# Gate copies placed together ahead of U loads, an uneven split of U tiles around a stage border, and the value stationary tiles in another pool

## The chip, the cores and the metric

One core of one Trainium2 chip. The metric is the device time of one execution in microseconds; times given for runs are medians of several executions.

## What is computed

One residual block over 512 tokens of width 1024, in float32. With RMSNorm in front of each part:

```
p  = xn @ W_in                        # 7 sections of 1024 columns
x  = x + W_out(sigmoid(ma)*ya + sigmoid(mb)*yb)      # two gated token mixers
q  = xn @ W_q ; top 16 of 128 sub-keys twice per head, top 16 of their sums   # 8 heads
x  = x + sum over the 128 chosen experts e of  g_e * gelu(<xn, U[e]>) * V[e]
out = RMSNorm(x)
```

There are 128 x 128 experts; U and V are tables of 16384 rows of 1024 floats (64 MB each). The changed part is the last sum.

## The kernel before

Tokens stand in four tiles of 128. The first token tile is done by gathering rows of U and V with indirect DMAs. The other three tiles (`NDT` = 3, 384 tokens) are done densely: for all 128 blocks of 128 experts, TensorE makes hidden values with U (**U tiles**, psum `ph`, function `h_mm`, lines 396 to 400), a gate matrix says which experts a token chose and with which weight, and TensorE multiplies gated hidden values with V (**V tiles**, psum `acc`, `v_mm`, lines 824 to 833).

A float32 product is made of three fp32r products: each operand is split in a rounded part (`hi`, ScalarE copy) and the rest (`lo`, a subtraction on VectorE), and hi\*hi, hi\*lo, lo\*hi are added (`mm3`, lines 144 to 149). A matrix product has a stationary operand, loaded into the array, and a moving one. In the tables of a profile the names behind `<-` are both. For `pin`, `pq`, `ph` the stationary tile is the weight (`hi_in`, `hi_q`, `hi_u` and their `lo`) and the normed input `a1h`, `a1l` moves; for `po` the merged mixers `mh`, `ml` are stationary, for `pgt` `waxh`, `waxl`; for `acc` `wh`, `wl` (384 columns, used 128 at a time) are stationary and `hi_v`, `lo_v` move.

**Pools.** A tile pool is a stretch of each partition. `const` and `strm` are made first and lie lowest; `fp` (stage 1), `gp`, `ha`, `qp`, `sp`, `op`, `dp` come above. `strm` holds `raw` (6 buffers, `RB`), `hi` and `lo` (3 each, `SB`). `wh` and `wl` (3 each, lines 844, 845) are in `dp`, near the end. The first two weight tiles of W_q are split into `strm`, the other fourteen into `qp` (line 500). In the built program the `strm` splits lie at bytes 78,912 to 103,488 of a partition, those of `qp` at 138,944 to 163,520, `mh` and `ml` at 129,504 to 162,272, `waxh` and `waxl` at 127,296 to 129,344, `wh` and `wl` at 207,488 to 216,704.

**The stage of the gate matrices** (lines 753 to 783). For each dense token tile `t_`, 8 steps: each step (`h_step(mid)`) starts a load of a U tile if fewer than `RB` raws are out, splits one U tile if fewer than `SB` are split, and in between (`mid`) makes 16 token columns of gate matrices on TensorE (`gate_mm`, psum `pg`), which ScalarE copies to `stg` (line 731), and one-hots for the next step on VectorE (`one_hot`); then one split U tile is multiplied (`h_run`) and its result goes through gelu (`hg`) and to DRAM (`hd`, line 406). `stg` has one buffer of 8 MB. Before the next token tile may write it, it must be copied to `gd` in DRAM: four DMAs of 2 MB in pieces of 512 bytes (line 776). Behind the 8 steps stand `HB[t_]` = 6 steps without gates, so that TensorE has work meanwhile; at each of the first four, one copy is started, then the step's load. The third tile is not copied (`HB` = 0); V tiles read it in `stg`. PE, ACT, DVE and POOL keep the order written (`pinned`); the DMA queue of SP is ordered by the tile framework. A DMA started on SP waits for what it needs, and all behind it on SP wait too.

**The stage of V tiles** (lines 838 to 869). 128 turns; each loads `raw_v`, splits it (ACT, then DVE `lo_v`), loads gates `gt` and, for the last 54, stored hidden values `hr`, makes `wf` (two products on DVE), `wh` (ACT), `wl` (DVE) and 18 matmuls. The first 68 turns also make a U tile of 24 matmuls. Gathers for the first token tile run along: ACT writes the index (`eix`, line 669), POOL issues the gather (line 364), DVE adds the row block (line 387). Order here is the framework's.

## Time and profile before

| | |
|---|---|
| median of 3 runs | 1645.08 us (1640.75 to 1645.50) |
| the profiled execution | 1639.71 us |
| its span, first to last instruction | 1637.9 us |
| TensorE (PE) busy | 1610.1 us, 98% |
| VectorE busy | 1266.4 us, 77% |
| ScalarE busy | 689.4 us, 42% |
| mean granted TensorE clock | 0.994 of full speed |
| gate stage, about | 565 to 795 us of the span |
| V stage, about | 800 us to the end |

Matmuls overlap: the profile's mean duration of one is longer than the distance from one start to the next, so distances are read from the starts in the timeline. `SPq`, `ACTq` are DMA starts on those queues; the time of such a row is how long the queue was held by the start. [...] "L812 <- X" names what ended a wait.

### The profile page before, as it was taken

The page shows a single profiled execution, that of the slowest core. Times are in us where ns is not written, and L with a number is a line of the kernel's source. Part 1 is how long each engine was busy: PE and PEld are TensorE (multiplying, and loading weights), DVE is VectorE, ACT ScalarE, POOL GpSimd, SP SyncE. Part 2 cuts the span into 40 slices and gives each one's busy share as a digit, 9 for nine tenths or more (in the row PEclk, how much of TensorE's full clock was granted, in tenths as well). Part 3 has the DMA queues.
Part 4 walks back from the last instruction along what each step waited for, and adds up shares of the span by engine and source line. Part 5 has one row for each costly group of instructions (what it writes and reads, how often), then busy time and mean ns, then how long its engine had stood idle before and what let it go on. Part 6 is the DMA issues. An engine that isn't in the chain of part 4 may idle for free.

```text
span 1637.9 us, 23565 instructions
## 1 busy us (share of the span) xinstructions
PE 1610.1 (98%) x8402; PEld 1415.1 (86%) x8402; DVE 1266.4 (77%) x2404; ACT 689.4 (42%) x1222; POOL 515.2 (31%) x379
## 2 busy tenths in 40 slices
PE   9999999999999999898999999999999999999997
PEld 8888888888899999898988888999888888788775
DVE  6666666636999996767788888888888888867767
ACT  7444444434333454444434333433343333433334
POOL 0000000004788820000044544545454444223331
PEclk9999999999999999999999999999999999999999
DMA  6222323334333357777499999999999999988883
GB/s 226 93 93 94 93 94 100 98 102 179 110 123 102 128 185 229 250 239 248 165 329 329 323 328 333 334 325 330 343 325 329 328 333 354 321 305 292 289 294 142
DMA packets 157878, 378.31 MB, mean 231 GB/s; under 512 B 14016, under 2 KB 78016, under 8 KB 157632
## 3 DMA queue, kind: packets, MB, share of 16 engines
q1 hardware_dynamic: 112544, 229.86, 41.3%
q0 software_dynamic: 36864, 134.23, 23.2%
q10 hardware_dynamic: 8352, 12.72, 2.2%
q8 instruction: 65, 1.06, 0.3%
q14 instruction: 53, 0.43, 0.1%
HBM read 345.17 MB, written 31.59 MB: 230 GB/s over the span
## 4 chain that ended last, share of the span: by engine, by line
PE 73%; issue 8%; DVE 7%; DMA 6%; POOL 4%; ACT 1%; SPq 0%; POOLq 0%; DVEq 0%; ACTq 0%
PE ph L147 9%; PE ph L149 9%; PE ph L148 9%; PE pin L149 6%; PE pin L147 6%; PE pin L148 6%; PE acc L830 6%; PE acc L833 6%; PE acc L829 6%; POOL rv L364 3%; DMA rv<-in_v_tab_dram,eix 3%; PE pq L147 2%; PE pq L149 2%; PE pq L148 2%; DMA gd<-stg 1%
## 5 line engine op out<-in xcount | busy, mean ns | idle before, releaser
L147 PE MATMUL ph<-a1h,hi_u 128*128 128x384 f32 x1024 | 347.1, 339 | 0.0
L149 PE MATMUL ph<-a1h,lo_u 128*128 128x384 f32 x1024 | 344.1, 336 | 0.4 <-POOL lo_u L108 0.4
L148 PE MATMUL ph<-a1l,hi_u 128*128 128x384 f32 x1024 | 343.3, 335 | 0.0
L830 PE MATMUL acc<-lo_v,wh 128*128 128x512 f32 x768 | 303.3, 395 | 3.6 <-DVE lo_v L108 3.5
L829 PE MATMUL acc<-hi_v,wh 128*128 128x512 f32 x768 | 303.2, 395 | 0.0
L364 POOL DMA_INDIRECT rv<-in_v_tab_dram,eix x128 | 170.3, 1331 | 271.2 <-ACT eix L669 230.8
L833 PE MATMUL acc<-hi_v,wl 128*128 128x512 f32 x768 | 242.8, 395 | 0.0
L364 POOL DMA_INDIRECT ru<-in_u_tab_dram,eix x120 | 164.0, 1366 | 218.9 <-ACT eix L669 182.1
L387 DVE SCALAR_TENSOR_TENSOR acc<-rv,w,acc 128x1024 f32<-128x1024 f32 x128 | 164.6, 1286 | 86.8 <-DMA rv<-in_v_tab_dram,eix 86.4
L107 ACT ACTIVATE hi_v<-raw_v 128x1024 fp32r<-128x1024 f32 x128 | 134.7, 1053 | 189.8 <-PE ph L148 177.2
L373 DVE SCALAR_TENSOR_TENSOR ru<-ru,t 128x1024 f32<-128x1024 f32 x128 | 155.5, 1223 | 58.7 <-DMA ru<-in_u_tab_dram,eix 58.2
L148 PEld LDWEIGHTS ph<-a1l,hi_u 128*128 128x128 f32 x1024 | 193.1, 189 | 3.2
L147 PEld LDWEIGHTS ph<-a1h,hi_u 128*128 128x128 f32 x1024 | 193.1, 189 | 3.1
L149 PEld LDWEIGHTS ph<-a1h,lo_u 128*128 128x128 f32 x1024 | 192.8, 188 | 0.7 <-POOL lo_u L108 0.7
L849 ACT ACTIVATE wh<-wf 128x384 fp32r<-128x384 f32 x128 | 67.0, 525 | 276.6 <-PE acc L830 185.1
L830 PEld LDWEIGHTS acc<-lo_v,wh 128*128 128x128 f32 x768 | 143.9, 187 | 38.5 <-DVE lo_v L108 6.9
L149 PE MATMUL pin<-a1h,lo_in 128*128 128x512 f32 x448 | 174.4, 389 | 0.3 <-POOL lo_in L108 0.3
L833 PEld LDWEIGHTS acc<-hi_v,wl 128*128 128x128 f32 x768 | 143.8, 187 | 35.5 <-DVE wl L850 0.3
L148 PE MATMUL pin<-a1l,hi_in 128*128 128x512 f32 x448 | 174.4, 389 | 0.0
L147 PE MATMUL pin<-a1h,hi_in 128*128 128x512 f32 x448 | 174.3, 389 | 0.0
L829 PEld LDWEIGHTS acc<-hi_v,wh 128*128 128x128 f32 x768 | 143.8, 187 | 32.1 <-ACT hi_v L107 0.2
L108 DVE TENSOR_TENSOR lo_v<-raw_v,hi_v 128x1024 fp32r<-128x1024 f32 x128 | 156.1, 1219 | 2.4 <-ACT hi_v L107 2.3
(199 smaller groups left out, 2475.5 us busy)
## 6 DMA issues: line engine op xcount, KB each, us to landing
raw_u<-in_uT_dram SPq DMA_DIRECT2D x128, 512.0 KB, 5.4
raw_v<-in_v_tab_dram SPq DMA_DIRECT2D x128, 512.0 KB, 5.9
raw_in<-in_w_in_dram SPq DMA_DIRECT2D x56, 512.0 KB, 3.4
gd<-stg SPq DMA_DIRECT2D x8, 2048.0 KB, 12.1
gt<-gd SPq DMA_DIRECT2D x128, 128.0 KB, 5.2
hd<-hg ACTq DMA_DIRECT2D x54, 192.0 KB, 2.5
hr<-hd SPq DMA_DIRECT2D x54, 192.0 KB, 5.4
raw_q<-in_w_q_dram SPq DMA_DIRECT2D x16, 512.0 KB, 3.2
```

What stands on the lines that cost most here:

```text
L107: act.activation(hi, raw, AF.Copy)
L108: lo_eng.tensor_tensor(lo, raw, hi, op=ALU.subtract)
L147: pe.matmul(pt, wh(k), xh(k), start=start and m == 0, stop=False)
L148: pe.matmul(pt, wh(k), xl(k), start=False, stop=False)
L149: pe.matmul(pt, wl(k), xh(k), start=False, stop=stop and m == n - 1)
L364: ins = pool.indirect_dma_start(out=rows, out_offset=None, in_=tab, in_offset=bass.IndirectOffsetOnAxis(ap=ix, axis=0))
L373: dq.append(lambda: dve.scalar_tensor_tensor(rows, rows, 1.0, t0, op0=ALU.mult, op1=ALU.mult, accum_out=d0[:, n:n + 1]))
L387: dq.append(lambda: dve.scalar_tensor_tensor(acc0, rows, w0[:, n:n + 1], acc0, op0=ALU.mult, op1=ALU.add))
L829: pe.matmul(accs[t][h], wh[:, ts], hi[:, hsl], start=first, stop=False)
L830: pe.matmul(accs[t][h], wh[:, ts], lo[:, hsl], start=False, stop=False)
L833: pe.matmul(accs[t][h], wl[:, ts], hi[:, hsl], start=False, stop=last)
L849: act.activation(wh, wf, AF.Copy)
```

## The change

Loads of U tiles are topped up to six raws from step 3 on (before: step 4) and again behind the 8 steps; then the four copies of `stg` are written one behind the other, ahead of the six steps without gates, and no more inside them. The first step of token tiles 1 and 2 splits no U tile; step 3 splits up to two. `wh` and `wl` are taken from `strm` instead of `dp`; by that the built program has them at bytes 103,488 to 112,704, and what lies above `strm` moves up by 9,216 bytes (the splits of `qp` to 148,160, `mh` and `ml` to 138,720, `waxh` to 136,512).

```diff
-        def h_step(mid):
+        def h_step(mid, splits=1):
             if len(raws) < RB:
                 h_load()
-            made = None
-            if len(nxt) < SB and raws:
+            made = []
+            while len(made) < splits and len(nxt) + len(made) < SB and raws:
                 k_, raw = raws.pop(0)
                 hi = strm.tile([P, D], F32R, tag="hi", name=f"hi_u{k_}", bufs=SB)
                 act.activation(hi, raw, AF.Copy)
-                made = k_, raw, hi
+                made.append((k_, raw, hi))
             mid()
-            if made:
-                k_, raw, hi = made
+            for k_, raw, hi in made:
                 lo = strm.tile([P, D], F32R, tag="lo", name=f"lo_u{k_}", bufs=SB)
...
-                if s2 >= 4 and len(raws) < RB:
+                if s2 >= 3 and len(raws) < RB:
                     h_load()
-                h_step(mid)
+
+                h_step(mid, 0 if t_ and s2 == 0 else 2 if s2 == 3 else 1)
                 gather_steps(GSTEP[(sub // 2) % len(GSTEP)], 2)
+            while t_ < NDT - 1 and len(raws) < RB:
+                h_load()
+            if t_ < NDT - 1:
+                for q4 in range(4):
+                    sl = slice(q4 * 32, (q4 + 1) * 32)
+                    sync.dma_start(gd[sl, :, t_ * P:(t_ + 1) * P].rearrange("i j t -> j i t"), stg[:, sl, :])
             for m in range(HB[t_]):
-
-                if m < 4:
-                    sl = slice(m * 32, (m + 1) * 32)
-                    sync.dma_start(gd[sl, :, t_ * P:(t_ + 1) * P].rearrange("i j t -> j i t"), stg[:, sl, :])
                 h_step(lambda: None)
...
-        wh = dp.tile([P, TD], F32R, tag="wh", name=f"wh{i}", bufs=3)
-        wl = dp.tile([P, TD], F32R, tag="wl", name=f"wl{i}", bufs=3)
+        wh = strm.tile([P, TD], F32R, tag="wh", name=f"wh{i}", bufs=3)
+        wl = strm.tile([P, TD], F32R, tag="wl", name=f"wl{i}", bufs=3)
```

The DMA queue of SP behind the first token tile, before (`stg0` is that tile's gate matrix, `raw_u112` the load of U tile 112; U tiles run from 74 to 127, then from 0):

```order
L101 DMA raw_u111_5886<-in_uT_dram 128x1024
L776 DMA gd_2933<-stg0_5302 128x32x128
L101 DMA raw_u112_5969<-in_uT_dram 128x1024
L776 DMA gd_2933<-stg0_5302 128x32x128
L101 DMA raw_u113_6004<-in_uT_dram 128x1024
L776 DMA gd_2933<-stg0_5302 128x32x128
L101 DMA raw_u114_6039<-in_uT_dram 128x1024
L776 DMA gd_2933<-stg0_5302 128x32x128
L101 DMA raw_u115_6074<-in_uT_dram 128x1024
L101 DMA raw_u116_6108<-in_uT_dram 128x1024
```

and with the change:

```order
L101 DMA raw_u111_5886<-in_uT_dram 128x1024
L777 DMA gd_2933<-stg0_5302 128x32x128
L101 DMA raw_u112_5968<-in_uT_dram 128x1024
L777 DMA gd_2933<-stg0_5302 128x32x128 x3
L101 DMA raw_u113_6006<-in_uT_dram 128x1024
L101 DMA raw_u114_6040<-in_uT_dram 128x1024
L101 DMA raw_u115_6074<-in_uT_dram 128x1024
L101 DMA raw_u116_6108<-in_uT_dram 128x1024
```

The loads of tiles 113 and 114 no more stand between copies; the load of 112, which waits for the buffer of tile 106, still stands behind the first. Behind the second token tile it is the same, with tiles 126, 127 and 0.

ScalarE's order from the last step without gates into the next token tile, before:

```order
L404 ACTIVATE hg110_6173<-ph110_6148 128x384
L406 DMA hd_2932<-hg110_6173 128x384
L742 ACTIVATE hi_u113_6179<-raw_u113_6004 128x1024
L731 ACTIVATE stg1_6176<-pg16_0_6181 128x128x4
L731 ACTIVATE stg1_6176<-pg16_1_6191 128x128x4
L731 ACTIVATE stg1_6176<-pg17_0_6201 128x128x4
L731 ACTIVATE stg1_6176<-pg17_1_6211 128x128x4
L404 ACTIVATE hg111_6256<-ph111_6231 128x384
L406 DMA hd_2932<-hg111_6256 128x384
L742 ACTIVATE hi_u114_6261<-raw_u114_6039 128x1024
```

and with the change:

```order
L404 ACTIVATE hg110_6173<-ph110_6148 128x384
L406 DMA hd_2932<-hg110_6173 128x384
L731 ACTIVATE stg1_6176<-pg16_0_6179 128x128x4
L731 ACTIVATE stg1_6176<-pg16_1_6189 128x128x4
L731 ACTIVATE stg1_6176<-pg17_0_6199 128x128x4
L731 ACTIVATE stg1_6176<-pg17_1_6209 128x128x4
L404 ACTIVATE hg111_6252<-ph111_6227 128x384
L406 DMA hd_2932<-hg111_6252 128x384
L742 ACTIVATE hi_u113_6255<-raw_u113_6006 128x1024
```

The split of tile 113 stands one step later, behind the first copies out of psum; with step 3 the order is one tile ahead again. The orders of PE and POOL are the same before and after, and so are those of ACT and DVE outside these steps but for the first two turns of the V stage.

## Rows read from the trace of the kernel before

**Rows 1.** The page's first part: busy time of TensorE, its share of the span, instructions.
```profile
PE 1610.1 (98%) x8402; PEld 1415.1 (86%) x8402; DVE 1266.4 (77%) x2404; ACT 689.4 (42%) x1222; POOL 515.2 (31%) x379
```

**Rows 2.** TensorE's groups of instructions by line, shapes kept apart: fp32r matmuls of 512 columns in four places of the program. Behind the bar: busy us, mean ns of one, idle before them.
```profile
L147 PE MATMUL pin<-a1h,hi_in 128*128 128x512 f32 x448 | 174.3, 389 | 0.0
...
L829 PE MATMUL acc<-hi_v,wh 128*128 128x512 f32 x768 | 303.2, 395 | 0.0
...
L147 PE MATMUL po<-hi_out,mh 128*128 128x512 f32 x64 | 25.2, 394 | 0.0
...
L147 PE MATMUL pgt<-xch,waxh 128*128 128x512 f32 x16 | 6.3, 396 | 0.0
```

**Rows 3.** TensorE's timeline (start us, duration us): the first and the 16th of a run of matmuls of W_q tile 1 (split in `strm`), the first and the 19th of one of a later tile (split in `qp`), and the first matmul of V turns 68 and 69, which are 18 matmuls apart.
```profile
390.15 0.39 PE L147 MATMUL pq<-a1h,hi_q 128*128 128x512 f32 x1
...
393.55 0.39 PE L147 MATMUL pq<-a1h,hi_q 128*128 128x512 f32 x1
...
422.89 0.39 PE L147 MATMUL pq<-a1h,hi_q 128*128 128x512 f32 x1
...
427.07 0.40 PE L147 MATMUL pq<-a1h,hi_q 128*128 128x512 f32 x1
...
1371.91 0.39 PE L829 MATMUL acc<-hi_v,wh 128*128 128x512 f32 x1
...
1376.11 0.39 PE L829 MATMUL acc<-hi_v,wh 128*128 128x512 f32 x1
```

**Rows 4.** TensorE's waits, the gate stage (560 to 800 us) and the V stage (800 us to the end): us in total, times, longest.
```profile
PE pg L728 <- ACT stg L731: 12.2, 2, 6.2
...
PE acc L830 <- DVE lo_v L108: 3.5, 4, 1.5
```

**Rows 5.** TensorE's timeline around its two long waits: first and last of 16 gate matmuls, the first gate matmul behind each wait, and a U matmul behind each (7th and 8th of its tile).
```profile
664.53 0.24 PE L728 MATMUL pg<-o,oij 128*128 128x128 f16 x1
...
665.41 0.22 PE L729 MATMUL pg<-o,oij 128*128 128x128 f16 x1
671.86 0.27 PE L728 MATMUL pg<-o,oij 128*128 128x128 f16 x1 [6.23 <-ACT stg L731]
...
675.55 0.37 PE L147 MATMUL ph<-a1h,hi_u 128*128 128x384 f32 x1
...
753.39 0.27 PE L728 MATMUL pg<-o,oij 128*128 128x128 f16 x1 [5.97 <-ACT stg L731]
...
757.40 0.41 PE L148 MATMUL ph<-a1l,hi_u 128*128 128x384 f32 x1
```

**Rows 6.** Windows: behind the first wait, and the first turns of the V stage without U tiles, in which the wait of 1.5 us of rows 4 lies.
```profile
670.00:675.00 5.00, 3.14 (x21) 3.14 (x21) 1.22 (x1) 3.33 (x6) 0.00 (x0) 0.50 0.96 319
...
1370.00:1410.00 40.00, 38.88 (x170) 31.27 (x170) 33.72 (x58) 14.36 (x29) 13.26 (x11) 1.00 0.99 371
```

**Rows 7.** The timeline of SP's DMA queue behind the first token tile: start, how long the start held the queue.
```profile
631.60 0.38 SPq L776 DMA_DIRECT2D gd<-stg  x1
...
640.94 7.93 SPq L101 DMA_DIRECT2D raw_u<-in_uT_dram  x1
648.92 1.20 SPq L776 DMA_DIRECT2D gd<-stg  x1
...
659.03 1.07 SPq L776 DMA_DIRECT2D gd<-stg  x1
```

**Rows 8.** ScalarE's timeline: the gelu of two U tiles running one behind the other, and the first copies of the next token tile's gates, which waited for the copies to DRAM, behind token tiles 0 and 1.
```profile
654.49 0.49 ACT L404 ACTIVATE hg<-ph 128x384 f32<-128x384 f32 x1 [2.20 <-PE ph L149]
...
658.65 0.49 ACT L404 ACTIVATE hg<-ph 128x384 f32<-128x384 f32 x1 [2.15 <-PE ph L149]
...
671.21 2.06 ACT L731 ACTIVATE stg<-pg 128x512 f32<-128x512 f32 x4 [10.54 <-DMA gd<-stg]
...
752.74 2.07 ACT L731 ACTIVATE stg<-pg 128x512 f32<-128x512 f32 x4 [10.29 <-DMA gd<-stg]
```

**Rows 9.** Windows while the copies run (last column: GB/s of the DMA engines): two in the middle of copies, one where a load follows a copy, one at the start of the first copy behind token tile 1.
```profile
644.00:650.00 6.00, 6.00 (x37) 6.00 (x36) 2.44 (x2) 1.55 (x2) 0.00 (x0) 1.00 1.13 351
...
660.00:662.00 2.00, 2.00 (x19) 2.00 (x17) 1.97 (x3) 0.67 (x1) 0.00 (x0) 1.00 1.02 195
...
714.00:720.00 6.00, 6.00 (x37) 6.00 (x36) 5.22 (x6) 1.93 (x3) 1.61 (x1) 1.00 0.90 273
...
726.00:734.00 8.00, 8.00 (x49) 8.00 (x48) 2.23 (x2) 3.04 (x4) 0.00 (x0) 1.00 1.12 361
```

**Rows 10.** The page's DMA issues: KB of one, median us from start to landing.
```profile
gd<-stg SPq DMA_DIRECT2D x8, 2048.0 KB, 12.1
...
hd<-hg ACTq DMA_DIRECT2D x54, 192.0 KB, 2.5
```

**Rows 11.** GpSimd's timeline in the V stage without U tiles: the first gather of each group of three (turns 96, 104, 108, 112, 116; a group belongs to four turns).
```profile
1483.17 3.56 POOL L364 DMA_INDIRECT rv<-in_v_tab_dram,eix  x1 [6.50 <-ACT eix L669]
...
1516.77 3.50 POOL L364 DMA_INDIRECT rv<-in_v_tab_dram,eix  x1 [7.46 <-ACT eix L669]
...
1533.61 3.62 POOL L364 DMA_INDIRECT rv<-in_v_tab_dram,eix  x1 [7.51 <-ACT eix L669]
...
1551.28 3.62 POOL L364 DMA_INDIRECT rv<-in_v_tab_dram,eix  x1 [8.37 <-ACT eix L669]
...
1568.64 3.62 POOL L364 DMA_INDIRECT rv<-in_v_tab_dram,eix  x1 [8.11 <-ACT eix L669]
```

## The prediction

> **What bounds the kernel now.** First the busy times: TensorE is busy 98% of the span [rows 1]; nothing else comes near. So time can come only from TensorE waiting less, or from its matmuls following each other faster. Its waits by stage show where the first is to be had: in the gate stage it waits 12.2 us in two waits, both for ScalarE's copy into `stg`; in the V stage 3.5 us in four, for `lo_v` [rows 4]. Then the groups by line for the second: matmuls of one form, fp32r with 512 columns, take 389 ns in the first stage and 394 to 396 ns in three other places [rows 2]. These durations overlap, so the timeline's starts give the true distance: 15 steps of W_q tile 1 take 3.40 us, 226.7 ns each; 18 steps of a later W_q tile 4.18 us, 232 ns; a V turn of 18 takes 4.20 us, 233 ns [rows 3]. I make the sum against the profiled execution's own 1639.7 us, which lies 5.4 below the median of the runs and 1.0 below the lowest.
>
> **The copies, and what waits for them.** ScalarE's first copy of the next token tile begins at 671.21 and 752.74, each released by the DMAs from `stg` [rows 8]; TensorE goes on 0.65 us later, at 671.86 and 753.39 [rows 5]. It had stopped at 665.5 and some 747.2, with all six psum buffers for gates full: waits of 6.23 and 5.97 us. Behind each it runs at the lower clock: the window granted 0.50 [rows 6]. The 16 gate matmuls and 6 U matmuls from 671.86 to 675.55 took 3.69 us. At full clock 16 gate matmuls take 0.94 (664.53 to 665.41 is 15 steps [rows 5]) and a U matmul 0.173 (a tile of 24 each 4.16 us [rows 8]), together 1.98, so 1.7 us are lost; likewise 753.39 to 757.40, 16 and 7, 4.01 instead of 2.15, so 1.9. The two places cost 12.2 + 3.6 = **15.8 us**.
>
> How much earlier do the copies land? They are 2.10 MB each [rows 10]. In the middle of copies the engines move 351 to 361 GB/s; where a load follows a copy, only 195 [rows 9]. SP's queue shows why the load comes there: its start is held 7.93 us, until the copy ahead has nearly drained, and the next copy starts at 648.92, the fourth at 659.03 [rows 7]. In the changed order the first copy and the load of tile 112 stand as before, so nothing moves up to about 644. Then three copies run on, 6.29 MB, and beside them four `hd` stores, one per U tile of 4.16 us, 0.79 MB: 7.08 MB at 351 GB/s are 20.2 us, landing at about 664.7 with 0.5 for the end of the last. TensorE needs that plus 0.65, against 665.5: no wait, or a tenth of a us. Behind token tile 1 the three copies begin at about 726, beside five stores: 7.27 MB at 352 are 20.7 us, landing 747.2, a wait of 0.6. I take 1.0 us for both together. A wait that short leaves the clock: in the V stage one of 1.5 us stands in a window with 1.00 granted [rows 4, 6]. The copies give 15.8 - 1.0 = **14.8 us**.
>
> The row of before shows no copy directly behind a copy. Bounds: 361 GB/s leaves no wait, so 15.8; 273, the slowest window with a copy alone [rows 9], lands them at 670.4 and 753.1, and saves 0.8 us. I take 351, since those windows hold the same copies in full run; the 273 is the first copy's start into an empty queue.
>
> **The uneven split.** It removes and adds no work, and it is needed: tile 113 lands behind the fourth copy, and ScalarE's split of it, if it still stood ahead of the copies into `stg`, would hold them for it. What is late next is that tile. Tiles 111 and 112 are split before, 4.16 us each, with 0.94 us of gates for each of the two halves of a step; tile 113 is wanted some 6 us after the fourth copy lands, and a load of 0.52 MB takes 1.5 us at 351 GB/s with 1.06 of ScalarE and 1.2 of VectorE behind it. I cost it at nothing; its cover is those two tiles, and without them it would be 2 to 4 us at each border. The second split at step 3 adds 1.2 us to VectorE there, which the step without one has saved.
>
> **`wh` and `wl` in `strm`.** No instruction is added or removed. The distance of 226.7 ns appears wherever the stationary tile lies in `strm`; 232 to 234 wherever it lies above [rows 2, 3]. The W_q tiles are the clean pair: one line, one moving operand, 5.5 ns apart, and only the pool of the stationary tile differs. They stand 33 us apart in one stage. So I expect V turns at 18 x 226.7 = 4.08 us, 0.12 less each. No row has a stationary tile at the new place (103 to 113 KB of the partition, just above the fast ones, below the slow `waxh` at 127), nor a low one with `hi_v` moving; so the bounds are 0 and 0.12 us a turn, and I take 0.12 because the new place touches the fast tiles.
>
> For the first 68 turns, with U tiles, TensorE stays the bound: 68 x 0.12 = 8.2; I keep 7.5, since `lo_v` is already now and then just late [rows 4]. The last 60 turns have a second limit. A gather feeds a sum on VectorE, behind which the next `wf`, `wh` and index stand, and the index releases the next gather: a ring of four turns. Groups of gathers start 33.6 us apart over two groups up to turn 104, which is 4 x 4.20 per group, TensorE's pace; then 16.84, 17.67 and 17.36, more than TensorE needs [rows 11]. At 4 x 4.08 = 16.3 TensorE would meet this ring earlier, from about turn 96. I count turns 77 to 96 (2.4 us) and nothing for the rest: **7.5 + 2.4 = 9.9 us**.
>
> **Sum:** 1639.7 - 14.8 - 9.9 = 1615.0. The runs shown lie 1 to 6 us above the profiled execution; I put the median 3 above: **1618 us**.
>
> **Rivals.**
>
> 1. The place of a stationary tile does nothing, and the 7 ns belong to something else of these stages (the moving operand, or what else reads SBUF). For it: `acc`, `po` and `pgt` also differ from `pin` in what moves. Against: the two kinds of W_q tiles. Time: 1618 + 9.9 = 1628. [...]
>
> 2. Copies behind each other run no faster than 273 GB/s (the descriptors of 512 bytes being the limit, not the loads between them). For it: the window at 714; against: 351 to 361 in the others [rows 9]. Saves 0.8 instead of 14.8: 1618 + 14 = 1632.
>
> 3. Slower: copies in one row are slower than the mix, because with loads among them the engines had reads to overlap. Place: the wait at the two borders. At 261 GB/s the copies land as late as now (7.08 MB from 644 to 671.1), and the gain of that part is gone; from about 221 GB/s the added waiting, 5 us at each border, eats the V stage's 9.9 us, and the kernel is slower. At the 195 of the window with a hand-over [rows 9] they land at 680.3 and 763.3: 15.5 and 16.7 us of wait instead of 6.2 and 6.0, 20 us more: 1639.7 + 20.0 - 9.9 = 1649.8, with the 3 above 1653. Against it: that window holds a load's start, not a copy's.
>
> 4. The ring of the V stage gives way (its gathers start earlier with TensorE, too) and the last 28 turns also gain 0.12 each, 3.4 us; with no wait left at the borders: 1618 - 3.4 - 1.0 = 1614.
>
> **How the numbers follow.** My forecast with rival 4, which is its other end (1610 to 1623): 0.64. Rival 1: 0.20 (1622 to 1632). Rival 2: 0.08 (1628 to 1636). Rivals 1 and 2 together, about 1642, which is no change: 0.05. Rival 3: 0.03. The range 1606 to 1633 holds the first two and half of the third, and 4 us below the forecast's end for a median nearer to the profile. Differences within 0.3% (5 us) of 1645 can't be told from none. Faster 0.92, same 0.05, slower 0.03.
>
> **What would show it.** Right: SP's queue shows four copies with one load between the first two; ScalarE's first copies of token tiles 1 and 2 are released within 1 us of TensorE's arrival; TensorE's waits for `stg` fall from 12.2 to under 2 us and no window of the gate stage grants 0.50; `acc` matmuls take 389 ns instead of 395 with 4.08 us per turn; waits for `lo_v` grow from 3.5 us to 5 to 9 in the last 40 turns. Wrong: `acc` still at 395 (rival 1); copies to DRAM landing after 668 (rival 2) or 671 (rival 3); a new wait of `ph` for tile 113 or 127, which would mean that the stock of split tiles was too small.

## The result and the profile of the changed kernel

The changed kernel takes **1634.8 us** (median of 6 runs, 1632.7 to 1639.2), the kernel before 1644.8 beside it (6 runs, 1640.8 to 1647.1): ratio 0.9945, 95% interval 0.9927 to 0.9964. That is 10 us faster where 27 were forecast, and just above the range's 1633. The profiled execution took 1635.9 with a span of 1634.1; the one before lay 5 below its kernel's median (1639.7), so the two traces lie only 3.8 apart.

The page's busy times of the changed kernel, and its `acc` groups by line, which answer [rows 1, 2]:

```profile
PE 1600.7 (98%) x8402; PEld 1413.2 (86%) x8402; DVE 1265.9 (77%) x2404; ACT 687.7 (42%) x1222; POOL 522.3 (32%) x379
```

```profile
L831 PE MATMUL acc<-hi_v,wh 128*128 128x512 f32 x768 | 299.7, 390 | 0.0
L832 PE MATMUL acc<-lo_v,wh 128*128 128x512 f32 x768 | 301.7, 393 | 10.7 <-DVE lo_v L108 10.6
L835 PE MATMUL acc<-hi_v,wl 128*128 128x512 f32 x768 | 239.0, 390 | 0.0
```

The mean of `acc<-hi_v,wh` fell from 395 to 390 as forecast. The starts of V turns 69 and 70, which answer [rows 3], are 4.08 us apart, to the digit the value predicted:

```profile
1373.24 0.39 PE L831 MATMUL acc<-hi_v,wh 128*128 128x512 f32 x1
...
1377.32 0.39 PE L831 MATMUL acc<-hi_v,wh 128*128 128x512 f32 x1
```

TensorE's waits, gate stage and V stage, which answer [rows 4]:

```profile
PE pg L728 <- ACT stg L731: 7.8, 2, 4.4
PE pg L728 <- DVE o L718: 3.1, 4, 0.8
...
PE acc L832 <- DVE lo_v L108: 10.6, 13, 2.2
PE ph L149 <- DVE lo_u L108: 1.3, 3, 0.5
```

and the waits for one-hots in the gate stage of the kernel before:

```profile
PE pg L728 <- DVE o L718: 1.3, 2, 0.8
```

Here the forecast broke. The waits for `stg` fell from 12.2 to 7.8, not to 1. Waits for one-hots (`o`) rose from 1.3 to 3.1 us. The waits for `lo_v` tripled from 3.5 to 10.6: 5.4 of them in the last 40 turns, where 5 to 9 were forecast, and 2.7 in the turns with U tiles, where none were. From turn 0 to turn 127 the V stage took 824.1 us in this execution and 823.1 in that of before, so nothing of what the shorter matmuls gave is left there. The waits of `ph` lie in the V stage (1029 to 1131 us), and none is for tile 113 or 127. ScalarE's first copies into `stg` behind the two borders, [rows 8], and the DMA queue of SP behind the first token tile, [rows 7]:

```profile
668.18 2.06 ACT L731 ACTIVATE stg<-pg 128x512 f32<-128x512 f32 x4 [9.25 <-DMA gd<-stg]
...
747.44 2.06 ACT L731 ACTIVATE stg<-pg 128x512 f32<-128x512 f32 x4 [10.24 <-DMA gd<-stg]
```

```profile
631.38 0.38 SPq L777 DMA_DIRECT2D gd<-stg  x1
635.38 4.01 SPq L101 DMA_DIRECT2D raw_u<-in_uT_dram  x1
639.43 17.44 SPq L777 DMA_DIRECT2D gd<-stg  x3
656.97 8.81 SPq L101 DMA_DIRECT2D raw_u<-in_uT_dram  x1
```

The order is the one intended, one load between the first two copies, and the copies land only 3.0 and 5.3 us earlier than before: 668.18 instead of 671.21, 747.44 instead of 752.74. Why is in the windows of the changed kernel (columns, as in [rows 6, 9]: length; busy time of TensorE, of its weight loads, of VectorE, ScalarE and GpSimd, each with the number of instructions; the granted TensorE clock as a share of full speed; the busy share of the DMA engines; GB/s):

```profile
643.00:650.00 7.00, 7.00 (x42) 7.00 (x42) 2.45 (x2) 2.31 (x3) 0.00 (x0) 1.00 1.11 354
652.00:656.00 4.00, 4.00 (x25) 4.00 (x25) 1.23 (x1) 1.40 (x3) 0.00 (x0) 1.00 0.97 300
656.00:660.00 4.00, 4.00 (x45) 3.84 (x44) 1.84 (x2) 0.73 (x2) 0.00 (x0) 1.00 0.99 297
660.00:664.00 4.00, 4.00 (x28) 4.00 (x26) 3.93 (x4) 0.00 (x0) 0.00 (x0) 1.00 0.97 296
...
745.00:752.00 7.00, 3.92 (x23) 3.91 (x23) 3.19 (x3) 4.11 (x8) 0.00 (x0) 0.54 0.94 321
```

Behind a load the copies run at 354 GB/s, as counted on, but from 652 on, copy behind copy, at about 297 with the `hd` stores in it. The kernel before has loads between the copies. Its first two windows here are the first copies behind token tiles 0 and 1, past their starts; the other three are later copies, each behind a load:

```profile
635.00:637.00 2.00, 2.00 (x14) 2.00 (x13) 1.78 (x2) 0.70 (x1) 0.00 (x0) 1.00 1.15 348
...
716.00:720.00 4.00, 4.00 (x25) 4.00 (x24) 3.25 (x4) 1.43 (x2) 1.61 (x1) 1.00 0.96 290
...
652.00:658.00 6.00, 6.00 (x37) 6.00 (x36) 2.45 (x2) 1.83 (x3) 0.00 (x0) 1.00 1.09 353
663.00:669.00 6.00, 2.63 (x26) 2.35 (x25) 5.02 (x5) 0.00 (x0) 0.00 (x0) 0.98 1.13 349
734.00:742.00 8.00, 8.00 (x68) 7.84 (x68) 3.07 (x3) 2.73 (x5) 0.00 (x0) 1.00 1.10 352
```

Among the second to fourth copies of a row, one that follows a load runs at some 350, and one that follows a copy at 290 to 300 with the stores in it. So taking the loads away gained little. The first copies do not fit a rule of the load alone: behind token tile 0 the first copy ran at 348, in both kernels, though its load had landed some 3 us before, and behind token tile 1 at 290, right behind two loads. What makes a copy fast stays open. TensorE goes on at 668.83 and 748.09, which answers [rows 5]:

```profile
665.20 0.22 PE L729 MATMUL pg<-o,oij 128*128 128x128 f16 x1
668.83 0.22 PE L728 MATMUL pg<-o,oij 128*128 128x128 f16 x1 [3.41 <-ACT stg L731]
...
743.46 0.22 PE L729 MATMUL pg<-o,oij 128*128 128x128 f16 x1
748.09 0.26 PE L728 MATMUL pg<-o,oij 128*128 128x128 f16 x1 [4.40 <-ACT stg L731]
```

Behind the first wait its clock stayed at full speed (1.00 granted from 669 to 672, the next gate matmuls 0.06 us apart); behind the second it fell (the window above grants 0.54, the part from 748 to 752 grants 0.50, answering [rows 6]).

**The V stage turn by turn.** A turn starts with every 18th `acc` matmul of the timeline. From these starts, for each execution profiled in this study (us; turns 0 to 67 make a U tile too, 68 to 123 don't; "sums kept" is explained with its experiment):

| kernel | turn 0 starts | turns 0 to 67 | turns 68 to 123 | median turn of each | waits for `lo_v` |
|---|---|---|---|---|---|
| before | 801.8 | 570.1 | 238.4 | 8.38, 4.20 | 3.5 |
| changed | 797.8 | 571.4 | 237.4 | 8.31, 4.08 | 10.6 |
| copies_only | 801.3 | 571.3 | 242.8 | 8.38, 4.20 | 6.4 |
| place_only | 803.5 | 566.2 | 240.6 | 8.31, 4.08 | 10.3 |
| contig | 788.5 | 567.8 | 238.7 | 8.31, 4.08 | 9.3 |
| pieces_1k | 788.3 | 567.8 | 236.3 | 8.31, 4.08 | 7.9 |
| even_split | 805.8 | 568.6 | 239.0 | 8.31, 4.08 | 9.4 |
| place_gp | 803.2 | 570.3 | 236.0 | 8.31, 4.08 | 8.4 |
| place_ha | 801.7 | 567.9 | 240.1 | 8.31, 4.08 | 9.4 |
| align_dp | 804.0 | 570.0 | 239.1 | 8.31, 4.08 | 11.1 |
| shift_strm | 799.7 | 572.1 | 240.4 | 8.38, 4.20 | 5.7 |
| before_stt (sums kept) | 802.7 | 576.7 | 235.2 | 8.38, 4.20 | 1.6 |
| stt_order (sums kept) | 799.5 | 566.5 | 228.5 | 8.31, 4.08 | 0.7 |
| both (sums kept) | 788.9 | 569.7 | 229.1 | 8.31, 4.08 | 2.8 |
| both_even (sums kept) | 786.6 | 569.5 | 229.1 | 8.31, 4.08 | 2.6 |
| both_even2 (sums kept) | 786.7 | 568.6 | 228.6 | 8.31, 4.08 | 1.8 |
| best (sums kept) | 793.7 | 570.6 | 229.6 | 8.31, 4.08 | 4.4 |
| aligned (sums kept) | 784.3 | 568.6 | 229.6 | 8.31, 4.08 | 1.2 |

The fourth column is the one to read. 56 turns of 4.20 are 235.2, of 4.08 they are 228.5. With the order of sums that the framework chose, all eleven kernels take 236 to 243, whichever turn TensorE could run; with the sums kept, they take just their turns. The 68 turns with a U tile show no such split: with turns of 8.31 they take 566.2 to 571.4 in the framework's order and 566.5 to 570.6 with the sums kept.

### The profile page after: what moved, and what is told of

Read it like the earlier page. It is cut to its first block, busy times and chain, and to the rows that moved or that the text cites. A ratio compares the mean times of both kernels' runs of the same rounds, so it can differ in the third digit from the quotient of the medians.

```text
span 1634.1 us, 23568 instructions
## 1 busy us (share of the span) xinstructions
PE 1600.7 (98%) x8402; PEld 1413.2 (86%) x8402; DVE 1265.9 (77%) x2404; ACT 687.7 (42%) x1222; POOL 522.3 (32%) x379
## 4 chain that ended last, share of the span: by engine, by line
PE 59%; DMA 15%; DVE 9%; issue 8%; POOL 4%; ACT 2%; SPq 2%; DVEq 0%; POOLq 0%; ACTq 0%
DMA ru<-in_u_tab_dram,eix 7%; PE pin L149 6%; PE pin L147 6%; PE pin L148 6%; PE ph L147 6%; PE ph L149 6%; PE ph L148 6%; PE acc L832 4%; PE acc L835 4%; PE acc L831 4%; DMA rv<-in_v_tab_dram,eix 4%; POOL rv L364 3%; DMA gd<-stg 2%; PE pq L147 2%; PE pq L149 2%
## 5 line engine op out<-in xcount | busy, mean ns | idle before, releaser
L832 PE MATMUL acc<-lo_v,wh 128*128 128x512 f32 x768 | 301.7, 393 | 10.7 <-DVE lo_v L108 10.6
L831 PE MATMUL acc<-hi_v,wh 128*128 128x512 f32 x768 | 299.7, 390 | 0.0
L364 POOL DMA_INDIRECT rv<-in_v_tab_dram,eix x128 | 176.8, 1381 | 264.6 <-ACT eix L669 215.0
L835 PE MATMUL acc<-hi_v,wl 128*128 128x512 f32 x768 | 239.0, 390 | 0.0
L387 DVE SCALAR_TENSOR_TENSOR acc<-rv,w,acc 128x1024 f32<-128x1024 f32 x128 | 164.5, 1285 | 82.7 <-DMA rv<-in_v_tab_dram,eix 82.5
```

The lines of the kernel that those rows point to most:

```text
L364: ins = pool.indirect_dma_start(out=rows, out_offset=None, in_=tab, in_offset=bass.IndirectOffsetOnAxis(ap=ix, axis=0))
L387: dq.append(lambda: dve.scalar_tensor_tensor(acc0, rows, w0[:, n:n + 1], acc0, op0=ALU.mult, op1=ALU.add))
L831: pe.matmul(accs[t][h], wh[:, ts], hi[:, hsl], start=first, stop=False)
L832: pe.matmul(accs[t][h], wh[:, ts], lo[:, hsl], start=False, stop=False)
L835: pe.matmul(accs[t][h], wl[:, ts], hi[:, hsl], start=False, stop=last)
```

## Experiments

My theory going in: the copies in a row are held by their pieces of 512 bytes; the place is worth what its matmuls say, but VectorE, standing at sums whose gathers have not landed, delivers `lo_v` late. Its rivals: DRAM writes run no faster than 290 GB/s; the V stage has a pace of its own that nothing here changes.

**Which part earned the 10 us.** copies_only is the changed kernel with its last lines taken back:

```diff
-        wh = strm.tile([P, TD], F32R, tag="wh", name=f"wh{i}", bufs=3)
-        wl = strm.tile([P, TD], F32R, tag="wl", name=f"wl{i}", bufs=3)
+        wh = dp.tile([P, TD], F32R, tag="wh", name=f"wh{i}", bufs=3)
+        wl = dp.tile([P, TD], F32R, tag="wl", name=f"wl{i}", bufs=3)
```

> The change without its last two lines: wh and wl stay in dp, copies and uneven split as changed. Theory A (the two parts are separate; the copies gain what the start of V turn 0 shows, 4.1 us, and the V stage stands as before): V turn 0 starts at 798, V turns 8.38 and 4.20 us, waits for lo_v 3 to 4 us, time 1640 to 1641 against 1645. Theory B (the V stage has a pace of its own, so that what is gained ahead of it is lost in it again): V turn 0 at 798 too, but more waits in the V stage, time 1644 to 1646.

Measured: 1643.2 (12 runs), ratio 0.9991 (0.9978 to 1.0005): no difference that can be told. Turn 0 starts at 801.3, not 798. Its waits for `stg` are 8.0 (3.5 and 4.5), nearly as in the changed kernel, but here the clock fell behind the first one (0.50 from 669 to 672), and in the changed kernel only behind the second. Behind the first wait, the changed kernel and this one:

```profile
669.00:672.00 3.00, 3.00 (x29) 3.00 (x27) 1.99 (x2) 2.38 (x5) 0.00 (x0) 1.00 0.96 348
```

```profile
669.00:672.00 3.00, 3.00 (x21) 3.00 (x21) 1.17 (x1) 2.50 (x5) 0.00 (x0) 0.50 0.94 363
```

In TensorE's waits 4.2 us are saved at `stg` and 1.8 lost at one-hots; 1.5 are left in the time. Neither theory's time came: there was hardly anything to pass on.

place_only is the reverse edit, on the kernel before:

```diff
-        wh = dp.tile([P, TD], F32R, tag="wh", name=f"wh{i}", bufs=3)
-        wl = dp.tile([P, TD], F32R, tag="wl", name=f"wl{i}", bufs=3)
+        wh = strm.tile([P, TD], F32R, tag="wh", name=f"wh{i}", bufs=3)
+        wl = strm.tile([P, TD], F32R, tag="wl", name=f"wl{i}", bufs=3)
```

> The kernel before with only wh and wl in strm. Both theories: acc matmuls with a median distance of 227 instead of 233 ns, start of V turn 0 at 802 as before. Theory A (the gain of the place is eaten by VectorE, where lo_v comes late behind sums that wait for gathers): waits for lo_v 10 to 11 us instead of 3.5, V stage from turn 0 to turn 127 816 to 818 us, time 1639 to 1645. Theory B (the changed kernel's late lo_v come from the earlier border, not from the place): waits for lo_v about 4 us, V stage about 808, time 1636 to 1637.

Measured: 1638.0 (11 runs), 0.9965 (0.9949 to 0.9980), 5.8 us faster; `lo_v` waits 10.3, turn 0 at 803.5. Theory A's waits, and a time just below its range (in the profiled execution turn 0 to turn 127 took 821.7, above the 816 to 818 expected). The two parts alone add up to 7.3 us against 9.0 (5.9 to 12.0) for the whole by its ratio, no contradiction within these intervals. So over half of what was gained came from the two lines on `wh` and `wl`, and of the reordering, the larger part of the diff, next to nothing by itself.

**What holds the copies.** contig is the changed kernel with another layout of `gd`:

```diff
-    gd = dram.tile([P, P, TG], F32, name="gd")
+    gd = dram.tile([NDT - 1, P, P, P], F32, name="gd")
...
-                    sync.dma_start(gd[sl, :, t_ * P:(t_ + 1) * P].rearrange("i j t -> j i t"), stg[:, sl, :])
+                    sync.dma_start(gd[t_, :, sl, :], stg[:, sl, :])
...
-        sync.dma_start(gt, gd[i])
+        sync.dma_start(gt.rearrange("j (a t) -> j a t", a=NDT - 1), gd[:, :, i, :].rearrange("a j t -> j a t"))
```

> The changed kernel with gd laid out so that a copy writes 16 KB in one piece per partition instead of 32 pieces of 512 bytes; the gate loads of the V stage then read 256 pieces of 512 bytes instead of 128 of 1 KB. Theory A (the small pieces hold copies behind each other at 290 GB/s): copies land as at 350 GB/s or faster, the last of them before 665 and 744, TensorE's waits for stg 8.3 us fall under 1 us, no window of the gate stage at the lower clock, V turn 0 starts at 788 to 790 instead of 797.8; time 1625 to 1630 if the V stage passes that on, 1634 if it has a pace of its own. Theory B (290 GB/s is what writing to DRAM gives, whatever the pieces): copies land at 668 and 747 as now, time 1634 to 1636.

Measured: 1624.1 (5 runs), 0.9877 (0.9858 to 0.9896). Windows of this kernel in the middle of copies, and all its waits in the gate stage:

```profile
640.00:656.00 16.00, 16.00 (x95) 16.00 (x94) 4.68 (x4) 5.83 (x8) 0.00 (x0) 1.00 1.02 429
720.00:732.00 12.00, 12.00 (x71) 12.00 (x71) 3.19 (x4) 4.67 (x6) 0.00 (x0) 1.00 1.02 427
```

```profile
PE pg L728 <- DVE o L718: 3.7, 5, 0.8
PE ph L149 <- POOL lo_u L108: 0.4, 1, 0.4
```

The same 8 MB, in the same order on the same queue, at 428 GB/s, with no wait for `stg` left; turn 0 starts 9.2 us earlier than in the changed kernel, and the time falls by 10.7. The V stage passes on what comes early. DRAM was not the limit. The edit changes where the pieces lie in DRAM together with their size; the two are not told apart: 290 GB/s at 512 bytes, 428 at 16 KB.

Is it the number of pieces, or their size? pieces_1k, with pairs of 512 bytes side by side:

```diff
+    gd = dram.tile([NDT - 1, P // 2, P, 2, P], F32, name="gd")
...
+                    sync.dma_start(gd[t_, q4 * 16:(q4 + 1) * 16].rearrange("i j b t -> j i (b t)"),
+                                   stg[:, sl, :].rearrange("j (i b) t -> j i (b t)", b=2))
```

> The changed kernel with gd laid out so that a copy writes pieces of 1 KB instead of 512 bytes, half as many. Theory A (what holds copies in a row at 290 GB/s is the number of pieces, some 566 a us, as in the window of 1133 packets in 2 us): copies in a row at over 400 GB/s, as with 16 KB, no wait for stg, 1623 to 1627. Theory B (a piece costs by its bytes and 16 KB is fast because a whole partition goes in one): 300 to 340 GB/s, waits for stg of 2 to 5 us left, 1628 to 1633.

Measured: 1625.5 (4 runs), 0.9887 (0.9873 to 0.9902), no wait for `stg`, but a window of 372, not over 400. It holds two rates, 389 in the second copy, behind a load, and 349 in the third, which follows a copy:

```profile
640.00:656.00 16.00, 16.00 (x94) 16.00 (x93) 4.44 (x4) 6.07 (x8) 0.00 (x0) 1.00 1.06 372
644.00:646.00 2.00, 2.00 (x13) 2.00 (x12) 0.93 (x1) 0.13 (x1) 0.00 (x0) 1.00 1.09 389
652.00:654.00 2.00, 2.00 (x14) 2.00 (x13) 1.23 (x1) 0.00 (x0) 0.00 (x0) 1.00 1.04 349
```

Theory A has the time, but neither theory the rate. A fixed number of pieces a us would have allowed twice 290. Why these copies are faster behind a load stays open; that larger pieces, laid out so, make them faster is shown, and 1 KB is enough here, since copies landed by 665 stop nobody.

even_split is the changed kernel without the uneven split:

```diff
-                h_step(mid, 0 if t_ and s2 == 0 else 2 if s2 == 3 else 1)
+                h_step(mid)
```

> The changed kernel with one U tile split at every step again. Theory A (as I wrote: tile 113 lands behind the fourth copy, and its split, standing ahead of the copies into stg, would hold them): ScalarE's first stg copy 2 to 3 us later at each border, waits for stg 13 to 15 us instead of 8, one-hots 2 us less; 1637 to 1642 against 1634.8. Theory B (the load runs beside the last copy and lands with it, so that the uneven split only costs its late one-hots): waits for stg as in the changed kernel, 1632 to 1634.

Measured: 1640.7 (12 runs), 0.9978 (0.9963 to 0.9992), 5.9 us slower than the changed kernel. ScalarE's split of tile 113 in this kernel:

```profile
672.07 1.06 ACT L742 ACTIVATE hi_u<-raw_u 128x1024 fp32r<-128x1024 f32 x1 [12.62 <-DMA raw_u<-in_uT_dram]
```

The waits for `stg` are 15.5 us, 1.3 for one-hots. Theory A: with copies this slow the uneven split is what saves the reordering; it takes 7.7 us of waits away and brings 1.8 in late one-hots.

**What holds the V stage.** In stt_order the sums of gathered rows (the two `scalar_tensor_tensor` of `gather_u` and `gather_v`) are kept on VectorE where the program writes them in the V stage, instead of where the framework moves them; no instruction is added or taken.

```diff
-        dq.append(lambda: dve.scalar_tensor_tensor(acc0, rows, w0[:, n:n + 1], acc0, op0=ALU.mult, op1=ALU.add))
+        dq.append(lambda: kept(dve.scalar_tensor_tensor(acc0, rows, w0[:, n:n + 1], acc0, op0=ALU.mult, op1=ALU.add)))
...
+    def kept(ins):
+        if keep[0]:
+            tc.keep_in_program_order(ins)
...
     rpool.append((dp, DR))
+    keep[0] = True
```

> The changed kernel with the sums of gathered rows of the V stage kept on VectorE where the program writes them, a turn or two later than the framework puts them. Theory A (lo_v is late because VectorE stands at a sum whose gather has not landed): waits for lo_v fall from 10.6 to under 4 us, V stage from 817 to 809 to 812, time 1627 to 1631. Theory B (the ring of gather, sum, index and next gather sets the pace of the last turns, and a later sum makes it longer): the waits move to other operands or stay, groups of gathers in the last turns 17 to 18 us apart, time 1634 to 1640.

Measured: 1624.2 (5 runs), 0.9882 (0.9864 to 0.9901): 10.6 us less than the changed kernel. It is theory A, with a time below its 1627 to 1631 and a V stage of 807.9 below its 809 to 812. VectorE's group of these sums, in the changed kernel and in this one, and TensorE's one kind of wait left in the V stage here (behind the second bar: VectorE's idle time ahead of a sum, and what ended it):

```profile
L387 DVE SCALAR_TENSOR_TENSOR acc<-rv,w,acc 128x1024 f32<-128x1024 f32 x128 | 164.5, 1285 | 82.7 <-DMA rv<-in_v_tab_dram,eix 82.5
```

```profile
L392 DVE SCALAR_TENSOR_TENSOR acc<-rv,w,acc 128x1024 f32<-128x1024 f32 x128 | 164.3, 1284 | 37.2 <-DMA rv<-in_v_tab_dram,eix 36.2 <-issue 0.6 <-DVE wf L856 0.3
```

```profile
PE acc L838 <- DVE lo_v L108: 0.7, 1, 0.7
```

VectorE had stood 82.7 us at sums whose rows were not there, with `lo_v` and `wf` behind them; now 37.2. GpSimd's gathers show the ring: in the changed kernel the first of a group of three takes 3.62 and the groups drift, 16.69 and 17.08 and 16.87 us apart, where four turns need 16.32, which answers [rows 11]; with the sums kept, nearly each takes 1.04, and they come in step with the turns (4.08, 8.16):

```profile
1480.29 3.62 POOL L364 DMA_INDIRECT rv<-in_v_tab_dram,eix  x1 [8.42 <-ACT eix L669]
...
1496.98 3.62 POOL L364 DMA_INDIRECT rv<-in_v_tab_dram,eix  x1 [8.45 <-ACT eix L669]
...
1514.06 3.62 POOL L364 DMA_INDIRECT rv<-in_v_tab_dram,eix  x1 [8.09 <-ACT eix L669]
...
1530.93 3.62 POOL L364 DMA_INDIRECT rv<-in_v_tab_dram,eix  x1 [7.91 <-ACT eix L669]
```

```profile
1472.84 1.04 POOL L364 DMA_INDIRECT rv<-in_v_tab_dram,eix  x1 [7.12 <-ACT eix L674]
1476.92 1.04 POOL L364 DMA_INDIRECT rv<-in_v_tab_dram,eix  x1 [3.04 <-ACT eix L674]
1481.00 1.04 POOL L364 DMA_INDIRECT rv<-in_v_tab_dram,eix  x1 [3.04 <-ACT eix L674]
1489.16 1.04 POOL L364 DMA_INDIRECT rv<-in_v_tab_dram,eix  x1 [7.12 <-ACT eix L674]
```

The same edit on the kernel before:

> The kernel before with only the sums of the V stage kept in program order. Theory A (late lo_v cost it the 3.5 us of its profile and little else; the sums become dear only at the shorter turns of the new place): 1640 to 1643. Theory B (the order of sums is worth 10 us by itself, whatever the turns): 1633 to 1636.

Measured: 1638.0 (5 runs), 0.9962 (0.9948 to 0.9975), some 6 us less: between the theories. The late sums cost the old kernel more than the 3.5 us of its profiled execution (copies_only, with the same turns, had 6.4 us of such waits), and the new one 4 us more than that. The execution profiled is the slowest of the five (1642.0). Its long turns 0 to 67 hold a wait of 1.84 us for `lo_u` at 1164.1, with the lower clock behind it, which no other execution of the table has between turn 0 and turn 127:

```profile
1164.60:1168.00 3.40, 3.40 (x12) 3.40 (x11) 3.19 (x4) 0.00 (x0) 0.38 (x1) 0.50 0.93 310
```

**Low in a partition, or something else?** The lines moved `wh` from byte 207,488 to 103,488. Two places in between, on the kernel before, `gp` and then `ha` in the place of `dp`:

```diff
-        wh = dp.tile([P, TD], F32R, tag="wh", name=f"wh{i}", bufs=3)
+        wh = gp.tile([P, TD], F32R, tag="wh", name=f"wh{i}", bufs=3)
...
```

> The kernel before with wh and wl in gp: wh at bytes 121,408 to 126,016 of a partition, wl at 126,016 to 130,624, between the fast place (under 112,704) and the slow ones (from 127,296). If the address decides, with its edge at 128 KB (131,072) or above, both are at 227 ns, and 390 mean; with an edge between 112,704 and 121,408 both are at 233, and 395; with an edge inside, wh is fast and wl slow. If the pool strm decides (what its neighbours are read for), both stay at 233.

> The kernel before with wh and wl in ha: wh at bytes 130,624 to 135,232 of a partition, wl at 135,232 to 139,840, just above the place that gave 227 ns (121,408 to 130,624). If there is an edge at 131,072, all but the first 448 bytes lie above it: 232 to 234 ns and a mean of 394 or 395. If the edge lies higher (the next slow tile known is at 138,944), wh is at 227 and wl partly: a mean of 390 for wh.

Both are fast (1637.8 and 1638.0, one run each; `acc<-hi_v,wh` has a mean of 390 in both, a turn 4.08), against the edge that I expected. At 131,072 to 139,840 `acc` takes 227 ns, while `W_q` tiles from 138,944 take 232. What the fast tiles have in common is the remainder of their first byte by 512: 64 for all of them (78,912, 103,488, 121,408, 130,624), and for all that moves there, `a1h`, `a1l` and `hi_v`, `lo_v`. The slow ones have 128 (`wh` before), 192 (`W_q` tiles), 480 (`mh`, `ml`). Two kernels turn height and remainder round: align_dp, the kernel before with two small tiles of 32 bytes (`ssf`, `ssg`) taken behind `wh` and not ahead of it, and shift_strm, the changed kernel with 32 bytes of padding in `strm`.

```diff
-    ssf = dp.tile([P, NTT, 2], F32, name="ssf")
-    ssg = dp.tile([P, NTT], F32, name="ssg")
+    fin = []
...
+        if t == 0:
+            fin.extend((dp.tile([P, NTT, 2], F32, name="ssf"), dp.tile([P, NTT], F32, name="ssg")))
```

```diff
+        if i == 0:
+            dve.memset(strm.tile([P, 8], F32, name="pad"), 0.0)
         wh = strm.tile([P, TD], F32R, tag="wh", name=f"wh{i}", bufs=3)
```

> The kernel before, wh and wl still in dp and high in a partition, but 64 bytes lower (207,424 to 216,640), since the two small tiles ssf and ssg are taken behind them instead of ahead. Theory C (not how high the stationary tile lies, but the remainder of its first byte by 512: it is 64 in all places that gave 227 ns, at 78,912, 103,488, 121,408 and 130,624, as it is for the moving tiles; 128 for wh of the kernel before at 207,488, 192 for the W_q tiles at 138,944, 480 for mh): acc at 227 ns and a mean of 390, time as with the place alone, 1636 to 1640. Theory A (height: fast up to about 140,000, slow above): 233 ns, 395, time 1643 to 1646.

> The changed kernel with 32 bytes of padding ahead of wh in strm, so that wh starts at 103,520 (remainder 96 by 512) instead of 103,488; wl and all above move up with it. Theory C: acc back at 231 to 237 ns, a mean of 394 to 396, time 1639 to 1643. Theory A: 227 ns, 390, time 1633 to 1636.

Measured: align_dp 1641.5 (12 runs), 0.9975 (0.9961 to 0.9988); shift_strm 1642.3 (12 runs), 0.9985 (0.9972 to 0.9997). Their groups:

```profile
L831 PE MATMUL acc<-hi_v,wh 128*128 128x512 f32 x768 | 299.7, 390 | 0.0
L835 PE MATMUL acc<-hi_v,wl 128*128 128x512 f32 x768 | 239.0, 390 | 0.0
```

```profile
L831 PE MATMUL acc<-hi_v,wh 128*128 128x512 f32 x768 | 303.2, 395 | 0.0
L835 PE MATMUL acc<-hi_v,wl 128*128 128x512 f32 x768 | 242.8, 396 | 0.0
```

High and aligned is fast, low and 32 bytes off is slow: theory C. The time of align_dp, 2.9 us less than before, falls short of the 1636 to 1640 expected; its trace has 11.1 us of waits for `lo_v`, the loss already known, and its interval overlaps that of place_only. The same was then tried on other slow tiles: best is the kernel both_even (below) with this:

```diff
+        dve.memset(qp.tile([P, 96], F32, name="pad"), 0.0)
         pool.iota(ic, pattern=[[1, NC]], base=0, channel_multiplier=0, allow_small_or_imprecise_dtypes=True)
...
+        dve.memset(fp.tile([P, 24], F32, name="pad"), 0.0)
         ml = fp.tile([P, KD, S], F32R, name="ml")
```

> The run both_even with padding of 384 bytes in qp and 96 bytes in fp, by which the fourteen W_q tiles, three U tiles, mh and ml start at a remainder of 64 by 512. Theory C: pq and po matmuls at 227 instead of 231 to 237 ns, some 336 x 5 and 192 x 6.5 ns, 2.9 us in all; on TensorE's path 1608 to 1610 against 1611.5. Theory A: no change of a matmul's distance, 1610 to 1613.

Measured: 1620.0 (5 runs). The distances came as expected, the time did not: the padding had been made by one more VectorE instruction, the first `lo_q` came behind it and behind eight sums for `a1l`, and TensorE waited 7.0 us for it and then ran at the lower clock for a while (mean granted clock 0.995, where both_even had 0.999). All `pq` tiles behind that and all `po` stand 227 ns apart.

**Put together.** both has the edits of contig and stt_order; both_even and its repetition both_even2 have that of even_split too; aligned has also this, with the same instructions in the same order:

```diff
-        ic = qp.tile([P, NC], F16, name="ic")
+        ic = qp.tile([P, 256], F16, name="ic")[:, :NC]
...
-            q = fp.tile([P, KD], F32, name="sp_q")
+            q = fp.tile([P, KD + 24], F32, name="sp_q")[:, :KD]
```

> The changed kernel with gd in whole pieces per partition and with the sums of gathered rows kept in program order, the two edits that gave 1624.1 and 1624.2 each. Theory A (the two losses are separate, one ahead of the V stage and one in it): 1612 to 1615, no wait for stg, waits for lo_v under 2 us, V turn 0 at 788, V stage 808. Theory B (the V stage has a pace of its own that both only approach): 1618 to 1624.

> As the run before, but every step of the gate stage splits one U tile at most again, as in the kernel before. Theory A (the second split of step 3 is what makes one-hots late on VectorE, and with copies landed 9 us early no split stands for its tile): waits for one-hots 1.3 us instead of 3.7, no new wait of ph, 1610 to 1613. Theory B (the split of tile 113 stands ahead of the first copies into stg and waits for its load, the reason that I gave for the uneven split): a wait for stg of 1 to 4 us at each border, 1614 to 1620.

> The run both_even with two tiles made larger (ic in qp by 412 bytes, q in fp by 96), so that every instruction stays and the W_q tiles, three U tiles, mh and ml start at a remainder of 64 by 512, without the extra VectorE instruction of the run before. Theory C, with the distances of that run (pq and po at 227): 336 pq matmuls by 5 ns and 192 po by 6.5 are 2.9 us; 1608 to 1610 against 1611.5. If VectorE sets the pace of the pq stage, its 1.7 are taken up by waits there, and 1610 to 1611 are left.

> The run both_even once more, on the same chip as the run aligned, to be compared with it: 1610 to 1613.

| kernel | us | runs | ratio to before |
|---|---|---|---|
| both | 1612.9 | 5 | 0.9813 (0.9800 to 0.9827) |
| both_even | 1611.5 | 5 | 0.9804 (0.9790 to 0.9817) |
| both_even2 | 1610.7 | 5 | 0.9803 (0.9786 to 0.9819) |
| aligned | 1609.3 | 5 | 0.9789 (0.9773 to 0.9805) |

The two gains add up (1624 and 1624 to 1613): two separate losses. With copies that land early the even split costs nothing any more: its one-hot waits fall from 3.7 to 1.8, and the 1.4 us between both and both_even lie within the intervals. The alignment starts turn 0 at 784.3 instead of 786.7, 2.5 of the 2.9 us expected; 1.4 are left at the end, with intervals that overlap. `po` in both_even and in aligned:

```profile
L148 PE MATMUL po<-lo_out,mh 128*128 128x512 f32 x64 | 25.5, 399 | 0.0
```

```profile
L148 PE MATMUL po<-lo_out,mh 128*128 128x512 f32 x64 | 24.9, 389 | 0.0
```

## Why the prediction was wrong

It forecast 1618 and got 1634.8: 16.8 too low. The sign was right; two terms of the sum were missed, and a third cost was set at nothing.

- **"Then three copies run on ... at 351 GB/s": this step failed, and is the larger part.** 14.8 us were forecast, copies_only gave 1.5 (a loss of 0.8 to a gain of 3.6). The windows of [rows 9] at 351 and 361 held copies behind a load; from the third copy on, the changed kernel ran at 298. With 298 in the prediction's own sum, 7.08 MB from 644 land at about 668.3, and ScalarE's copy came at 668.18 (the 0.5 us for the end of the last copy, in this sum as in the forecast's, is an estimate of mine that no run shows by itself). I put the 273 aside as "the first copy's start", but its last four us, at 290, were no start. The rows of before did not settle it, since the other first copy ran at 348, so the low rate deserved more than a small chance. Rival 2 (512 bytes are the limit, not the loads) named this and had 0.08; contig (428 GB/s) and pieces_1k (349 and 389) bear it out. Its sign, a landing after 668, came. Its time, 1632, lies within 3 us in part by luck, as it kept the V stage's 9.9. Rival 3's reading, that a row is slower than the mix, came true as well, but short of the 261 GB/s from which it would have cost the gain.
- **The V stage: the distance was right, its worth was not.** 9.9 us were forecast, place_only gave 5.8 (3.3 to 8.4). In the turns without U tiles a turn of 4.08 came true, and by the table the last 56 turns gained about 2 us on average, near the 2.4 that I had counted there; single executions of one kind lie over 4 us apart. With the sums kept they gain 5.6 to 6.7, so VectorE, which keeps its order and stands at sums for their rows (82.7 us in the changed kernel), is the second limit there. In the 68 others I took 7.5. A turn there shrank by 0.07, not 0.12 (the first nine distances behind each U tile stay at 224 to 236 ns, 231 on average), so 4.8 us. Of these about half came: the eight kernels with turns of 8.31 average 568.7 over these 68, the three with 8.38 (before, copies_only, shift_strm) 571.2. Waits for `lo_v` and `lo_u`, 2.7 and 1.3 us in the changed kernel, stand in these turns, so "TensorE stays the bound" was too simple; but the six with the sums kept average 568.9, so the order of sums is not the cause, which stays open.
- **The uneven split "at nothing".** It brought 1.8 us of waits for one-hots. Its purpose was read rightly: without it, even_split lost 5.9.
- **Clock.** Where the waits for `stg` were to vanish, the clock's 3.6 us were to come back with them. With waits of 3.4 and 4.4 us left, the clock fell behind the second border in the changed kernel (0.50 granted from 748 to 752) and behind the first in copies_only (0.50 from 669 to 672), and the gain fell with it.
- **The cause of the short matmul** was wrong, though its result came out: not the pool, not the height, but the remainder of the first byte, which differs between the two kinds of W_q tiles too. Had the new place started 32 bytes further, nothing would have been gained there; that it did not was luck. Rival 1 (the place does nothing) fell: in shift_strm 32 bytes cost 5 ns of 390 a matmul.
- **Two readings of its own were off,** without weight for the forecast: at 273 GB/s its landing behind token tile 1 (753.1) is later than the 752.74 of before, so that bound saves 0.4, not 0.8; and by the waits of [rows 5] TensorE had stopped at 665.63 and 747.42, not at 665.5 and 747.2.
- **What was right:** that these two losses were there to be had, as the last four kernels show. With the copies really fast and the sums out of the way, the forecast's events all come true (no wait for `stg`, no low clock in the gate stage, the mean granted clock being 0.999, 4.08 a turn). Their 1613 lies below the forecast of 1618 because keeping the sums is worth 6 us in the kernel before too. Against before_stt, on the same chip, both is 25.0 us faster, where 24.7 were forecast: a match of the sum more than of its parts, since in the two traces turn 0 starts 13.7 earlier (14.8 forecast), and the turns 68 to 123 give 6.1 (2.4 forecast).

## What to carry to other kernels

Before taking a transfer rate from a window, look at what stood ahead of it in the queue, and take the rate from the stretch whose neighbours are those of the new order; where none has them, keep the slowest as a bound. A load between small-piece copies may be helping them (some 350 GB/s behind a load and 290 to 300 behind a copy here). When one engine is made faster in a stage that is 98% busy, list the in-order engine that feeds it and see at which instructions it stands waiting, since its stalls, hidden until then, can take back the gain (here 10.6 us of waits for `lo_v`, 0.7 with the sums kept). And when a matmul runs at two distances (here 227 and 233 ns), compare the first bytes of its tiles before anything else.

## What the runs showed of the hardware

- **Start of a stationary tile.** An fp32r matmul of 512 columns followed the one before at 227 ns where stationary and moving tile both start at a remainder of 64 by 512 (`acc` in the changed kernel, place_gp, place_ha and align_dp, W_q tile 1 in the kernel before, `pq` and `po` in best), and at 231 to 237 ns on average with the stationary at 96 (`acc` in shift_strm), 128, 192 or 480 (`acc`, the later W_q tiles and `po` in the kernel before). In shift_strm, where the 32 bytes put `mh` and `ml` at 0, `po` stands 226 to 232 ns apart. Behind a U tile the first nine distances of `acc` average 231 even at 64 (changed kernel). Whether the remainder itself counts or only that the two are equal, and by which modulus, was not tried; 256 would fit as well (`waxh`, 64 by 256 and slow, does not decide it, since `xch`, which moves there, starts at 32).
- **Copies to DRAM by size of piece:** from SBUF, with 512 bytes, 290 to 300 GB/s directly behind a copy and some 350 behind a load (first copies: 348 and 290), in the changed kernel and the one before; with 1 KB 349 and 389 (pieces_1k); with 16 KB 428 (contig).
- **The start of a gather on GpSimd** took 0.94 (changed kernel) to 1.04 us (stt_order) in most cases in the turns without U tiles, or 3.6 for the first of a group where the sums stood in the framework's place (3.62 in the changed kernel). What beside it makes it long was not tried.
- **Waits and the clock.** Waits of 3.4 and 3.5 us at the same place left the clock at full speed in one execution (1.00 granted from 669 to 672) and dropped it in another (0.50), and the same later gate matmul came 2.8 us later there (700.30 in the changed kernel, 703.08 in copies_only). In before_stt a wait of 1.84 us was followed by 3.4 us at 0.50.
